# The last LayerNorm of a decoder layer: its mean taken from row sums of the last weights, its squares on ScalarE

## The chip, the cores and the metric

The kernel runs on one core of a Trainium2 chip. The metric is the time of one execution on the device in microseconds (us), the median of several runs. Profiles are single executions; their span runs from the first to the last instruction, and the execution's own time is a little longer.

## What is computed

One post-norm decoder layer on 256 positions of width 1024, in float32. The change touches its end: the down projection of the feed-forward block and the second LayerNorm.

```python
u = causal_dwconv(x @ w_up[l], conv_w_ffn[l])
f = (jax.nn.silu(u[..., :D_FF]) * u[..., D_FF:]) @ w_down[l]
x = layer_norm(DEEPNORM_ALPHA * x + f, ln2_g[l], ln2_b[l])
```

`layer_norm` subtracts the mean of the 1024 columns, multiplies by the inverse root of the variance plus 1e-5, then by a gain `g`, and adds a bias `b`. D_FF is 2816, that is 22 tiles of 128 rows of `w_down`.

## The kernel before

All weights stream in as chunks of 1 MB into three `raw` buffers (SP issues the transfers, L175). A chunk holds two units of 128x1024 numbers. Each unit is split into a high half `wh` (ScalarE, `split_h`, L192) and a low half `wl` (VectorE, `split_l`, L197), and every matrix product is three float32r matmuls: high by high, high by low, low by high (`mm3`, L305 to L307).

In the feed-forward stage `slot` runs through a list `seq` of units. A unit's two halves are made some four or five places ahead of the matmuls that read them, with the convolution, SiLU and split of the activations (`FFN`, stages 0 to 3, L817 to L851) between them. The results are the f tiles, high and low half, read as weights by the down projection. Every engine works through its queue in order, in the order in which the program issues.

The down projection accumulates four PSUM banks `dacc[t][nh]`, two blocks of 128 positions (t) by two halves of 512 columns (nh). The last eight units (`TAIL`) are taken apart: `finish(0)` multiplies them into block 0 with a slot after each; then, on VectorE, block 0 is normed: two `residual` calls (L757 adds alpha times x1, L759 takes statistics), `norm_stats` (L735 mean and variance on VectorE, L736 power of -0.5 on GpSimd), and `norm_apply` twice (L740, L741), each followed by an output transfer on SP (L997). While VectorE does this, TensorE goes on with `finish(1)`: the eight units into columns 0 to 511 of block 1, then, by `down_part`, into columns 512 to 767 and last into 768 to 1023, each in a bank of its own (`e`). `dacc[1][1]` has the earlier units' part of columns 512 to 1023. VectorE adds each bank to the residual (L990) and takes statistics (L991). After the last of them come mean and variance (L735), the power (L736), the first step (subtract the mean, multiply by g, L747) and the second step (multiply by the inverse root, add b, L744) with two output transfers, 640 columns issued by SP and 384 by ScalarE's queue (L1003). `ln2` holds g and b in SBUF.

Of the kernel before, what the change touches and what calls it, by code (L numbers as in the profile page):

```python
# [24 lines left out]
NP = DFF // P  # L25
ALPHA = 2.0 ** 0.25
EPS = 1e-5
# [22 lines left out]
CHUNK = 2048  # L50
# [3 lines left out]
TAIL = 8  # L54
# [83 lines left out]
def layer_kernel(ctx: ExitStack, tc: tile.TileContext, x, wpack, cpack, ln1_g, ln1_b, ln2_g, ln2_b, out):  # L138
    nc = tc.nc

    cst = ctx.enter_context(tc.tile_pool(name="cst", bufs=1))
    big = ctx.enter_context(tc.tile_pool(name="big", bufs=1))
    wp = ctx.enter_context(tc.tile_pool(name="wp", bufs=1))
    tmp = ctx.enter_context(tc.tile_pool(name="tmp", bufs=1))
# [5 lines left out]
    def acc_bank(name):  # L150
        return psum.tile([P, 512], F32, tag="acc", name=name)
# [4 lines left out]
    def scratch(shape, name, bufs=None, tag="scr"):  # L156
        return tmp.tile(shape, F32, tag=tag, name=name, bufs=bufs or 6)
# [4 lines left out]
    RAW_BUFS, HL_BUFS = 3, 9  # L162
    chunks, plan_units, U = plan()
# [5 lines left out]
    def issue_dma(c):  # L169
        while len(raws) <= c and len(raws) < len(chunks):  # L170
# [5 lines left out]
            if i == XR_CHUNK:  # L176
                nc.sync.dma_start(xr, x[0].rearrange("(t p) d -> p t d", p=P))

    def alloc(u, part, tag):
        k, n = units[u]["shape"]  # L180
        units[u][part] = wp.tile([P, k, n], F32R, tag=tag, name=f"{tag}{u}", bufs=HL_BUFS)
# [6 lines left out]
    def split_h(u):  # L188

        issue_dma(units[u]["chunk"] + RAW_BUFS - 1)  # L190
        alloc(u, "h", "wh")
        nc.scalar.activation(units[u]["h"], raw_of(u), AF.Copy)  # L192

    def split_l(u):

# [3 lines left out]
    def raw_of(u):  # L199
        un = units[u]  # L200
        k, n = un["shape"]
        return raws[un["chunk"]][:, un["off"]:un["off"] + k * n].rearrange("p (k n) -> p k n", k=k)
# [15 lines left out]
    def hl_split(h, l, src, eng=None):  # L218
        nc.scalar.activation(h, src, AF.Copy)  # L219
        (eng or nc.vector).tensor_tensor(l, src, h.bitcast(F32), op=ALU.subtract)  # L220
# [25 lines left out]
    neghalf = cst.tile([P, 1], F32, name="neghalf")  # L246
    nc.gpsimd.memset(neghalf, -0.5)
    neghalf2 = cst.tile([P, 1], F32, name="neghalf2")
    invf = cst.tile([P, 8], F32, name="invf")
    for i, f in enumerate(INV_FREQ):  # L250
        nc.gpsimd.memset(invf[:, i:i + 1], f)
# [7 lines left out]
    xT = big.tile([P, KT, 2, S], F32R, tag="xT", name="xT")  # L259
# [12 lines left out]
    cs = cst.tile([P, 2, 2, 8], F32, name="cs")  # L272
# [375 lines left out]
    for j in range(16):  # L648
        u = U[("g", 0)] + j
# [26 lines left out]
    def ps_pair(name):  # L676
        return pairs.tile([P, 2, 512], F32, tag="pair", name=name)
# [54 lines left out]
    def norm_stats(r, stats, pieces):  # L732

        mv = tmp.tile([P, 4], F32, tag="mv", name="mv", bufs=4)
        nc.vector.bn_aggr(mv[:, 0:2], stats[:, 0:pieces, :])  # L735
        nc.gpsimd.tensor_tensor(mv[:, 3:4], mv[:, 1:2], neghalf, op=ALU.pow)  # L736
        return mv

    def norm_apply(o, r, mv, g, b):
        nc.vector.scalar_tensor_tensor(o, r, mv[:, 0:1], g, op0=ALU.subtract, op1=ALU.mult)  # L740
        nc.vector.scalar_tensor_tensor(o, o, mv[:, 3:4], b, op0=ALU.mult, op1=ALU.add)  # L741

    def norm_second(r, mv, ln, cs):
        nc.vector.scalar_tensor_tensor(r[:, cs], r[:, cs], mv[:, 3:4], ln[:, 1, cs], op0=ALU.mult, op1=ALU.add)  # L744

    def norm_first(r, mv, ln, cs):
        nc.vector.scalar_tensor_tensor(r[:, cs], r[:, cs], mv[:, 0:1], ln[:, 0, cs], op0=ALU.subtract, op1=ALU.mult)  # L747

    x1 = big.tile([P, 2, D], F32, tag="rows", name="x1")
    x1T = big.tile([P, KT, 2, S], F32R, tag="xT", name="x1T")  # L750

# [4 lines left out]
    def residual(t, nh, bank, res, r, stats, piece, c0, c1):  # L756
        nc.vector.scalar_tensor_tensor(r[:, c0:c1], res[:, t, c0:c1], ALPHA, bank[:, c0 - nh * 512:c1 - nh * 512],  # L757
                                       op0=ALU.mult, op1=ALU.add)
        nc.vector.bn_stats(stats[:, piece, :], r[:, c0:c1])  # L759
        if piece == 0:  # L760
            with_eps(stats)
# [19 lines left out]
        residual(0, nh, banks[nh], xr, r1[0], st1[0], nh, nh * 512, nh * 512 + 512)  # L781
    norm1(0, r1[0], st1[0])
    nc.scalar.activation(neghalf2, neghalf, AF.Silu)
    banks = [acc_bank(f"o1{nh}") for nh in range(2)]
    for k in range(4):
        wo_rows(k, 1, banks)
# [14 lines left out]
    ln2 = big.tile([P, 2, D], F32, tag="e8", name="ln2")  # L801
# [6 lines left out]
    def f_tile(i):  # L808
        g = i // 8
        if g not in FT:  # L810
            FT[g] = big.tile([P, 8, 2, S], F32R, tag=("b16", "c16", "b16")[g], name=f"f{g}")
        return FT[g][:, i % 8]
# [62 lines left out]
    b0, r0 = up0_rows(0)  # L875
# [15 lines left out]
    dacc = [[acc_bank(f"d{t}{nh}") for nh in range(2)] for t in range(2)]  # L891

    def down(i, ts=(0, 1), nhs=(0, 1)):
        un = units[U[("dn", i // 2)] + i % 2]
        ft = f_tile(i)
        for t in ts:
            for nh in nhs:
                mm3(dacc[t][nh], ft[:, 0, t * P:(t + 1) * P], ft[:, 1, t * P:(t + 1) * P],
                    un["h"][:, 0, nh * 512:(nh + 1) * 512], un["l"][:, 0, nh * 512:(nh + 1) * 512],
                    i == 0, i == NP - 1 or (t == 1 and nh == 1 and i == NP - TAIL - 1))  # L900

    def down_part(i, bank, c):
        un = units[U[("dn", i // 2)] + i % 2]
        ft = f_tile(i)
        mm3(bank[:, 0:256], ft[:, 0, P:2 * P], ft[:, 1, P:2 * P],
            un["h"][:, 0, c * 256:(c + 1) * 256], un["l"][:, 0, c * 256:(c + 1) * 256], i == NP - TAIL, i == NP - 1)


    pending = []

    def take(n):
        out = []
        for stage, i in list(pending):
            if len(out) < n and i not in [p for _, p in out]:
                out.append((stage, i))
                pending.remove((stage, i))
        return out
# [49 lines left out]
        slot(k, stages)  # L967


    def finish(t):  # L970
        r = x1[:, t]
        stats = tmp.tile([P, 4, 6], F32, tag="stats", name=f"rstats{t}", bufs=2)
        if t == 0:
            for k in range(TAIL):
                down(NP - TAIL + k, (t,))
                slot(tail_from + k, take(2))
            assert not pending
            for nh in range(2):
                residual(t, nh, dacc[t][nh], x1, r, stats, nh, nh * 512, nh * 512 + 512)
        else:  # L980
            for i in range(NP - TAIL, NP):
                down(i, (t,), (0,))
            nc.vector.scalar_tensor_tensor(r[:, 512:1024], x1[:, t, 512:1024], ALPHA, dacc[t][1], op0=ALU.mult, op1=ALU.add)
            for c in range(2):
                residual(t, 0, dacc[t][0], x1, r, stats, c, c * 256, c * 256 + 256)
            for c in range(2, 4):
                bank = ps_pair(f"e{c}")[:, 0]
                for i in range(NP - TAIL, NP):
                    down_part(i, bank, c)
                nc.vector.tensor_tensor(r[:, c * 256:c * 256 + 256], r[:, c * 256:c * 256 + 256], bank[:, 0:256], op=ALU.add)  # L990
                nc.vector.bn_stats(stats[:, c, :], r[:, c * 256:c * 256 + 256])  # L991
        mv = norm_stats(r, stats, 2 if t == 0 else 4)
        if t == 0:
            for c in range(2):
                cc = slice(c * 512, (c + 1) * 512)
                norm_apply(r[:, cc], r[:, cc], mv, ln2[:, 0, cc], ln2[:, 1, cc])
                nc.sync.dma_start(out[0, t * P:(t + 1) * P, cc], r[:, cc])  # L997
            return
        for c in range(2):
            norm_first(r, mv, ln2, slice(c * 512, c * 512 + 512))  # L1000
        for cc, queue in ((slice(0, 640), nc.sync), (slice(640, D), nc.scalar)):
            norm_second(r, mv, ln2, cc)
            queue.dma_start(out[0, t * P:(t + 1) * P, cc], r[:, cc])  # L1003

    for t in range(2):
        finish(t)


_INS = ['x', 'ln1_g', 'ln1_b', 'ln2_g', 'ln2_b']
# [39 lines left out]
```

## Time and profile before

| | us |
|---|---|
| median of 3 runs | 367.78 |
| lowest and highest run | 367.34, 368.45 |
| the profiled execution | 367.38 |
| its span | 365.6 |

PE is TensorE's matmul, PEld its weight load, DVE is VectorE, ACT is ScalarE, POOL is GpSimd, SP is SyncE. Rows of a timeline give the start in us from the beginning of the span, the length in us, the engine, the line of the kernel, the operation, the tile written and those read with their shapes, and in brackets how long the engine had been idle and what released it. Instructions on one engine overlap at their edges, so the distance from one start to the next can be less than a length.

### The profile page before, as it was taken

The page shows a single profiled execution, that of the slowest core. Times are in us where ns is not written, and L with a number is a line of the kernel's source. Part 1 is how long each engine was busy: PE and PEld are TensorE (multiplying, and loading weights), DVE is VectorE, ACT ScalarE, POOL GpSimd, SP SyncE. Part 2 cuts the span into 40 slices and gives each one's busy share as a digit, 9 for nine tenths or more (in the row PEclk, how much of TensorE's full clock was granted, in tenths as well). Part 3 has the DMA queues.
Part 4 walks back from the last instruction along what each step waited for, and adds up shares of the span by engine and source line. Part 5 has one row for each costly group of instructions (what it writes and reads, how often), then busy time and mean ns, then how long its engine had stood idle before and what let it go on. Part 6 is the DMA issues. An engine that isn't in the chain of part 4 may idle for free.

```text
span 365.6 us, 5224 instructions
## 1 busy us (share of the span) xinstructions
PE 356.8 (98%) x1964; PEld 309.4 (85%) x1964; DVE 296.8 (81%) x510; ACT 222.7 (61%) x380; POOL 13.5 (4%) x34
## 2 busy tenths in 40 slices
PE   8999999999999999999999999999999999999991
PEld 8888888888898888888888888888888888888891
DVE  4885888779986669989769888977768697999884
ACT  4775777576977666653357676664737475767400
POOL 2000000000000003401100000000000000000000
PEclk9999999999999999999999999999999999999997
DMA  8988465335645634588160845447180917663011
GB/s 270 348 296 329 166 230 192 135 117 199 261 163 183 232 115 127 223 331 287 69 230 20 326 136 210 158 189 277 68 329 24 331 57 295 231 229 117 2 57 57
DMA packets 11240, 69.61 MB, mean 190 GB/s; under 512 B 1232, under 2 KB 1616, under 8 KB 4176
## 3 DMA queue, kind: packets, MB, share of 16 engines
q1 hardware_dynamic: 10496, 67.00, 49.6%
q0 software_dynamic: 576, 2.10, 1.7%
q8 instruction: 15, 0.25, 0.3%
q10 hardware_dynamic: 144, 0.20, 0.1%
q14 instruction: 9, 0.07, 0.1%
HBM read 68.24 MB, written 1.05 MB: 190 GB/s over the span
## 4 chain that ended last, share of the span: by engine, by line
PE 98%; DVE 1%; DVEq 0%; issue 0%
PE pb L323 20%; PE pb L330 10%; PE g L323 8%; PE d L305 5%; PE d L306 5%; PE d L307 5%; PE g L330 4%; PE y L323 4%; PE q L546 3%; PE k L546 3%; PE v L546 3%; PE b L323 2%; PE y L330 2%; PE c L323 2%; PE o L305 2%; PE o L307 2%
## 5 line engine op out<-in xcount | busy, mean ns | idle before, releaser
L197 DVE TENSOR_TENSOR wl<-raw,wh 128x1024 fp32r<-128x1024 f32 x99 | 121.1, 1225 | 26.2 <-ACT wh L192 25.8
L192 ACT ACTIVATE wh<-raw 128x1024 fp32r<-128x1024 f32 x99 | 103.6, 1054 | 28.0 <-DMA raw<-in_wpack 28.0
L323 PE MATMUL pb<-x1T,wh 128*128 128x512 f32 x320 | 76.2, 390 | 0.0
L323 PEld LDWEIGHTS pb<-x1T,wh 128*128 128x128 f32 x320 | 59.7, 188 | 12.1
L330 PEld LDWEIGHTS pb<-x1T,wl 128*128 128x128 f32 x320 | 41.0, 191 | 1.6
L330 PE MATMUL pb<-x1T,wl 128*128 128x256 f32 x320 | 41.5, 283 | 0.0
L220 DVE TENSOR_TENSOR wl<-raw,wh 128x1024 fp32r<-128x1024 f32 (+1 forms) x29 | 27.3, 982 | 7.8 <-ACT wh L219 7.5
L323 PE MATMUL g<-xT,wh 128*128 128x512 f32 x128 | 31.7, 394 | 0.0
L305 PE MATMUL d<-wh,f 128*128 128x512 f32 x80 | 31.3, 391 | 0.0
L306 PE MATMUL d<-wl,f 128*128 128x512 f32 x80 | 31.3, 391 | 0.0
L307 PE MATMUL d<-wh,f 128*128 128x512 f32 x80 | 31.1, 389 | 0.0
L219 ACT ACTIVATE wh<-raw 128x1024 fp32r<-128x1024 f32 (+1 forms) x29 | 23.7, 860 | 10.7 <-DMA raw<-in_wpack 6.6
L323 PEld LDWEIGHTS g<-xT,wh 128*128 128x128 f32 x128 | 23.2, 189 | 4.4
L835 DVE SCALAR_TENSOR_TENSOR fc<-fb,consts,fc 128x254 f32<-128x254 f32 x40 | 19.3, 483 | 1.4
L833 DVE SCALAR_TENSOR_TENSOR fc<-fb,consts,fc 128x255 f32<-128x255 f32 x40 | 19.1, 477 | 0.0
L827 ACT ACTIVATE fc<-fb,consts 128x256 f32<-128x256 f32 x40 | 18.0, 497 | 1.7 <-DVE fb L821 1.7
L817 ACT ACTIVATE fb<-pb 128x512 f32<-128x512 f32 x20 | 11.8, 589 | 9.9 <-PE pb L330 9.8
L307 PEld LDWEIGHTS d<-wh,f 128*128 128x128 f32 x80 | 15.0, 188 | 3.2
L305 PEld LDWEIGHTS d<-wh,f 128*128 128x128 f32 x80 | 15.1, 189 | 2.7
L306 PEld LDWEIGHTS d<-wl,f 128*128 128x128 f32 x80 | 15.1, 189 | 2.6
L330 PEld LDWEIGHTS g<-xT,wl 128*128 128x128 f32 x128 | 16.4, 191 | 0.6
L330 PE MATMUL g<-xT,wl 128*128 128x256 f32 x128 | 16.6, 283 | 0.0
(181 smaller groups left out, 576.8 us busy)
## 6 DMA issues: line engine op xcount, KB each, us to landing
raw<-in_wpack SPq DMA_DIRECT2D x55, 1024.0 KB, 5.0
raw<-in_wpack SPq DMA_DIRECT2D x6, 896.0 KB, 5.9
xr<-in_x SPq DMA_DIRECT2D x1, 1024.0 KB, 7.6
ln<-in_ln_g POOLq DMA_DIRECT2D x2, 512.0 KB, 5.5
ln<-in_ln_b POOLq DMA_DIRECT2D x2, 512.0 KB, 6.1
raw<-in_wpack SPq DMA_DIRECT2D x3, 256.0 KB, 3.2
raw<-in_wpack SPq DMA_DIRECT2D x1, 512.0 KB, 5.8
out<-x SPq DMA_DIRECT2D x2, 256.0 KB, 2.0
```

Source lines behind the costliest of these rows:

```text
L192: nc.scalar.activation(units[u]["h"], raw_of(u), AF.Copy)
L197: nc.vector.tensor_tensor(units[u]["l"], raw_of(u), units[u]["h"].bitcast(F32), op=ALU.subtract)
L219: nc.scalar.activation(h, src, AF.Copy)
L220: (eng or nc.vector).tensor_tensor(l, src, h.bitcast(F32), op=ALU.subtract)
L305: nc.tensor.matmul(o, ah, bh, start=start, stop=False)
L306: nc.tensor.matmul(o, ah, bl, start=False, stop=False)
L307: nc.tensor.matmul(o, al, bh, start=False, stop=stop)
L323: nc.tensor.matmul(bank, un["h"][:, k, n0:n0 + P], b[:, k].rearrange("p a s -> p (a s)"), start=k == 0, stop=False)
L330: nc.tensor.matmul(bank[:, 0:S], un["l"][:, k, n0:n0 + P], b[:, k, 0], start=False, stop=k == nk - 1)
L546: nc.tensor.matmul(banks[m][t], (xl if p == 2 else xh)[:, k, t * P:(t + 1) * P], wl if p == 1 else wh, start=k == 0 and p == 0, stop=k == ...
L833: nc.vector.scalar_tensor_tensor(c[:, 1:S], pb[:, a * S:a * S + S - 1], w_ffn(1, j), c[:, 1:S], op0=ALU.mult, op1=ALU.add)
L835: nc.vector.scalar_tensor_tensor(c[:, 2:S], pb[:, a * S:a * S + S - 2], w_ffn(0, j), c[:, 2:S], op0=ALU.mult, op1=ALU.add)
```

## The change

Block 1's sum over the last 256 columns is taken without waiting for these columns. The sum over columns of a product equals the product with the sums of the weights' rows.

- For each of the last eight units ScalarE, behind the high half, copies columns 768 to 1023 of the raw weights with an accumulator; the accumulator output is the row sum.
- After the last slot ScalarE multiplies the eight f tiles (block 1, high and low part) by their row sums into `fs`. GpSimd adds the 16 tiles in five instructions; its power for block 0 stands after the second. ScalarE and VectorE split the total into two float32r tiles, `fsr`.
- Two matmuls with a constant of ones, after the sixth matmul of the last column group, sum `fsr` over its rows into `mean`.
- VectorE makes the residual of block 1 in three parts, with row sums as accumulator output where a part is complete: columns 512 to 767, 768 to 1023 (without the last eight units) and 0 to 511. The order is after block 0's norm, as before; statistics are no longer taken there.
- After the mean, ScalarE squares the first two parts with the mean as bias, with accumulators; VectorE subtracts the mean from them and multiplies by g, into a new tile `res`; it subtracts the mean from the last part.
- After the last bank: one add, one multiply-and-sum instruction that starts from the other parts' sum, the power on GpSimd, and beside it the multiplication of the last part by g. Then the second step and the two transfers as before, from `res`.

```diff
+    LAST_UNITS = [U[("dn", i // 2)] + i % 2 for i in range(NP - TAIL, NP)]
+    rowsum = cst.tile([P, TAIL], F32, name="rowsum")
...
         nc.scalar.activation(units[u]["h"], raw_of(u), AF.Copy)
+        if u in LAST_UNITS:
+            j = LAST_UNITS.index(u)
+            nc.scalar.activation(scratch([P, 256], f"rowsum{j}", tag="gs", bufs=3), raw_of(u)[:, 0, 768:1024], AF.Copy,
+                                 accum_out=rowsum[:, j:j + 1])
...
+    nc.gpsimd.memset(ones32, 1.0)
...
+    nc.scalar.activation(ones, ones32, AF.Copy)
...
-            for c in range(2, 4):
-                bank = ps_pair(f"e{c}")[:, 0]
-                for i in range(NP - TAIL, NP):
-                    down_part(i, bank, c)
-                nc.vector.tensor_tensor(r[:, c * 256:c * 256 + 256], r[:, c * 256:c * 256 + 256], bank[:, 0:256], op=ALU.add)
-                nc.vector.bn_stats(stats[:, c, :], r[:, c * 256:c * 256 + 256])
...
-        for c in range(2):
-            norm_first(r, mv, ln2, slice(c * 512, c * 512 + 512))
-        for cc, queue in ((slice(0, 640), nc.sync), (slice(640, D), nc.scalar)):
-            norm_second(r, mv, ln2, cc)
-            queue.dma_start(out[0, t * P:(t + 1) * P, cc], r[:, cc])
...
+    fs = big.tile([P, TAIL, 2, P], F32, tag="d8", name="fs")
+    for j in range(TAIL):
+        nc.scalar.activation(fs[:, j], f_tile(NP - TAIL + j)[:, :, P:2 * P].bitcast(F32), AF.Copy, scale=rowsum[:, j:j + 1])
+
+    def fs_add(a, b):
+        nc.gpsimd.tensor_tensor(a, a, b, op=ALU.add)
+
+    fs_add(fs[:, 0:2], fs[:, 4:6])
+    fs_add(fs[:, 2:4], fs[:, 6:8])
...
+    mv = norm_stats(r0, stats, 2)
+    fs_add(fs[:, 0:2], fs[:, 2:4])
+    fs_add(fs[:, 0], fs[:, 1])
+    fs_add(fs[:, 0, 0], fs[:, 0, 1])
+    for c in range(2):
+        cc = slice(c * 512, (c + 1) * 512)
+        norm_apply(r0[:, cc], r0[:, cc], mv, ln2[:, 0, cc], ln2[:, 1, cc])
+        nc.sync.dma_start(out[0, 0:P, cc], r0[:, cc])
...
+    cols3 = (slice(0, 512), slice(512, 768), slice(768, D))
...
+    for c in (1, 2, 0):
+        bank = dacc[1][1][:, 256 * c - 256:256 * c] if c else dacc[1][0]
+        nc.vector.scalar_tensor_tensor(part[c], x1[:, 1, cols3[c]], ALPHA, bank, op0=ALU.mult, op1=ALU.add,
+                                       accum_out=None if c == 1 else sums[:, c:c + 1])
+    fsr = big.tile([P, 2, P], F32R, tag="xT", name="fsr")
+    hl_split(fsr[:, 0], fsr[:, 1], fs[:, 0, 0])
+    bank = ps_pair("e2")[:, 0]
+    for i in range(NP - TAIL, NP):
+        down_part(i, bank, 2)
+    nc.vector.scalar_tensor_tensor(part[1], bank[:, 0:256], 1.0, part[1], op0=ALU.mult, op1=ALU.add, accum_out=sums[:, 1:2])
+    nc.vector.tensor_reduce(sums[:, 3:4], sums[:, 0:3], axis=mybir.AxisListType.X, op=ALU.add)
+    bank = ps_pair("e3")[:, 0]
+    mean = acc_bank("mean")
+    for i in range(NP - TAIL, NP):
+        down_part(i, bank, 3)
+        if i == NP - TAIL + 1:
+            for part_hl in range(2):
+                nc.tensor.matmul(mean[:, 0:2], fsr[:, part_hl], ones, start=part_hl == 0, stop=part_hl == 1)
+
+    for c, f in ((4, -1.0 / D), (5, -1.0 / (32 * D))):
+        nc.vector.tensor_scalar(sums[:, c:c + 1], mean[:, 0:1], sums[:, 3:4], f, op0=ALU.add, op1=ALU.mult)
+    res = wp.tile([P, CHUNK], F32, tag="raw", name="res", bufs=RAW_BUFS)
+    for c in range(2):
+        nc.scalar.activation(scratch([P, 512], f"sq{c}")[:, 0:cols3[c].stop - cols3[c].start], part[c], AF.Square,
+                             bias=sums[:, 5:6], scale=1.0 / 32, accum_out=sums[:, 6 + c:7 + c])
+        nc.vector.scalar_tensor_tensor(res[:, cols3[c]], part[c], sums[:, 4:5], ln2[:, 0, cols3[c]], op0=ALU.add, op1=ALU.mult)
+    nc.vector.tensor_scalar(part[2], part[2], sums[:, 4:5], None, op0=ALU.add)
+    nc.vector.tensor_scalar(sums[:, 8:9], sums[:, 6:7], sums[:, 7:8], EPS, op0=ALU.add, op1=ALU.add)
+    nc.vector.tensor_tensor(part[2], part[2], bank[:, 0:256], op=ALU.add)
+    nc.vector.tensor_tensor_reduce(out=scratch([P, 256], "sq2"), in0=part[2], in1=part[2], scale=1.0 / D, scalar=sums[:, 8:9],
+                                   op0=ALU.mult, op1=ALU.add, accum_out=sums[:, 9:10])
+    nc.gpsimd.tensor_tensor(sums[:, 10:11], sums[:, 9:10], neghalf, op=ALU.pow)
+    nc.vector.scalar_tensor_tensor(res[:, cols3[2]], part[2], 1.0, ln2[:, 0, cols3[2]], op0=ALU.mult, op1=ALU.mult)
+    for cc, queue in ((slice(0, 640), nc.sync), (slice(640, D), nc.scalar)):
+        nc.vector.scalar_tensor_tensor(res[:, cc], res[:, cc], sums[:, 10:11], ln2[:, 1, cc], op0=ALU.mult, op1=ALU.add)
+        queue.dma_start(out[0, P:2 * P, cc], res[:, cc])
```

More of the change, by code (lines that the diff above doesn't have):

```diff
@@ L248, in layer_kernel @@
     neghalf2 = cst.tile([P, 1], F32, name="neghalf2")
+    ones32 = cst.tile([P, 2], F32, name="ones32")
+    nc.gpsimd.memset(ones32, 1.0)
+    ones = cst.tile([P, 2], F32R, name="ones")
     invf = cst.tile([P, 8], F32, name="invf")
@@ L741, in norm_apply @@
         nc.vector.scalar_tensor_tensor(o, o, mv[:, 3:4], b, op0=ALU.mult, op1=ALU.add)
[L743 to L747, printed above, removed]
     x1 = big.tile([P, 2, D], F32, tag="rows", name="x1")
@@ L967, in layer_kernel @@
         slot(k, stages)
[L970 to L980, printed above, removed]
-            for i in range(NP - TAIL, NP):
-                down(i, (t,), (0,))
-            nc.vector.scalar_tensor_tensor(r[:, 512:1024], x1[:, t, 512:1024], ALPHA, dacc[t][1], op0=ALU.mult, op1=ALU.add)
-            for c in range(2):
-                residual(t, 0, dacc[t][0], x1, r, stats, c, c * 256, c * 256 + 256)
-            for c in range(2, 4):
-                bank = ps_pair(f"e{c}")[:, 0]
-                for i in range(NP - TAIL, NP):
-                    down_part(i, bank, c)
[L990 to L999, printed above, removed]
-            norm_first(r, mv, ln2, slice(c * 512, c * 512 + 512))
-        for cc, queue in ((slice(0, 640), nc.sync), (slice(640, D), nc.scalar)):
-            norm_second(r, mv, ln2, cc)
-            queue.dma_start(out[0, t * P:(t + 1) * P, cc], r[:, cc])
@@ L1005, in layer_kernel @@
-    for t in range(2):
-        finish(t)
+    for k in range(TAIL):
+        down(NP - TAIL + k, (0,))
+        slot(tail_from + k, take(2))
+    assert not pending
+    fs = big.tile([P, TAIL, 2, P], F32, tag="d8", name="fs")
[5 more added lines that the diff above has]
+    fs_add(fs[:, 2:4], fs[:, 6:8])
@@ new lines, in layer_kernel @@
+    r0 = x1[:, 0]
+    stats = tmp.tile([P, 4, 6], F32, tag="stats", name="rstats", bufs=2)
+    for nh in range(2):
+        residual(0, nh, dacc[0][nh], x1, r0, stats, nh, nh * 512, nh * 512 + 512)
+    mv = norm_stats(r0, stats, 2)
[6 more added lines that the diff above has]
+        nc.sync.dma_start(out[0, 0:P, cc], r0[:, cc])
@@ new lines, in layer_kernel @@
+    cols3 = (slice(0, 512), slice(512, 768), slice(768, D))
+    part = [scratch([P, cc.stop - cc.start], f"part{c}") for c, cc in enumerate(cols3)]
+    sums = tmp.tile([P, 12], F32, tag="sums", name="sums", bufs=1)
+    for i in range(NP - TAIL, NP):
+        down(i, (1,), (0,))
+    for c in (1, 2, 0):
+        bank = dacc[1][1][:, 256 * c - 256:256 * c] if c else dacc[1][0]
+        nc.vector.scalar_tensor_tensor(part[c], x1[:, 1, cols3[c]], ALPHA, bank, op0=ALU.mult, op1=ALU.add,
+                                       accum_out=None if c == 1 else sums[:, c:c + 1])
@@ new lines, in layer_kernel @@
+    fsr = big.tile([P, 2, P], F32R, tag="xT", name="fsr")
[7 more added lines that the diff above has]
+    mean = acc_bank("mean")
+    for i in range(NP - TAIL, NP):
+        down_part(i, bank, 3)
+        if i == NP - TAIL + 1:
+            for part_hl in range(2):
+                nc.tensor.matmul(mean[:, 0:2], fsr[:, part_hl], ones, start=part_hl == 0, stop=part_hl == 1)
```

## The prediction

> **What bounds the kernel now.** I read the page first (busy time and the chain of waits), then the end of the chain in order of time, then the timeline of each engine from 318 us on.
>
> ```profile
> span 365.6 us, 5224 instructions
> PE 356.8 (98%) x1964; PEld 309.4 (85%) x1964; DVE 296.8 (81%) x510; ACT 222.7 (61%) x380; POOL 13.5 (4%) x34
> PE 98%; DVE 1%; DVEq 0%; issue 0%
> ```
>
> TensorE sets the pace until its last matmul; nothing the change does elsewhere counts before that, unless TensorE has to wait for it. After that matmul the chain belongs to VectorE:
>
> ```profile
> 357.84 0.43 DVE x L990
> 358.29 0.44 DVE rstats L991
> 358.75 0.27 DVE mv L735
> 359.05 1.45 DVE x L747 x2
> 360.59 0.89 DVE x L744
> 361.48 0.53 DVEq L1045
> ```
>
> Columns are start, length, what. From the last matmul's result (357.84) to the first second-step instruction that feeds an output transfer (360.59) are 2.75 us: add the bank, statistics, mean and variance, first step over all 1024 columns, and only then the second step. The second step and the two transfers stay as they are, so only these 2.75 us can shrink. The last two column groups on TensorE, and the moment at which VectorE sees a finished bank:
>
> ```profile
> 351.89 0.28 PE L305 MATMUL e<-wh,f 128*128 128x256 f32 x1
> 354.64 0.28 PE L307 MATMUL e<-wh,f 128*128 128x256 f32 x1
> 354.96 0.42 DVE L990 TENSOR_TENSOR x<-x,e 128x256 f32<-128x256 f32 x1 [0.34 <-PE e L307]
> 355.36 0.28 PE L307 MATMUL e<-wh,f 128*128 128x256 f32 x1
> 355.48 0.28 PE L305 MATMUL e<-wh,f 128*128 128x256 f32 x1
> 357.52 0.28 PE L307 MATMUL e<-wh,f 128*128 128x256 f32 x1
> ```
>
> The 24 matmuls of the first group start at 351.89 to 354.64, one per 0.12 us. The bank is visible 0.04 us after the last has ended (354.64 + 0.28 = 354.92, used at 354.96). The new mean matmuls stand after six matmuls of the last group, that is ahead of the one at 355.48: this is the time by which their operand must be there.
>
> **The new end, step by step.** Call s the time when VectorE sees the last bank (357.84 before). After the change it then does: one add (next dependent start 0.45 later, as 357.84 to 358.29), the square-and-sum with its accumulator read, the power on GpSimd, the second step. The square-and-sum is the operation that the attention masks use:
>
> ```profile
> 54.70 0.42 DVE L401 CUSTOM_DVE_ANT_0 sm<-s,mask 128x256 f32<-128x256 f32 x1
> 55.04 0.08 DVE L401 DVE_READ_ACCUMULATOR2_ANT st<- 128x1 f32 x1
> 359.09 0.55 POOL L736 TENSOR_TENSOR mv<-mv,neghalf 128x1 f32<-128x1 f32 x1 [9.32 <-DVE mv L735]
> 175.31 0.75 DVE L740 SCALAR_TENSOR_TENSOR x<-xr,mv,ln 128x512 f32<-128x512 f32 x1
> 175.36 1.12 POOL L736 TENSOR_TENSOR mv<-mv,neghalf 128x1 f32<-128x1 f32 x1 [9.33 <-DVE mv L735]
> 176.52 0.75 DVE L741 SCALAR_TENSOR_TENSOR x<-x,mv,ln 128x512 f32<-128x512 f32 x1 [0.46 <-POOL mv L736]
> ```
>
> It and its read take 0.42 in all (54.70 to 55.12), so the variance is there at s + 0.87. The power starts 0.07 later (mean and variance 358.75 + 0.27 = 359.02, power 359.09) and takes 0.55; the consumer starts 0.04 after it (175.36 + 1.12 = 176.48, then 176.52). That puts the second step at s + 1.53. But the scaling by the gain runs on VectorE beside the power, reading two SBUF tensors, and in the rows at 175 such an instruction held the power until it ended at 176.06; the power then needed 0.42. The scaling would end no later than s + 1.21, giving s + 1.67 at worst. I take 1.65: 2.75 - 1.65 = **1.10 us gained**, bounds 1.08 and 1.22.
>
> For that to hold, both partial squares must be summed before s. The mean matmul ends near 355.48 + 0.12 + 0.28 = 355.88; two one-element instructions lead to about 356.2. ScalarE then squares 512 and 256 columns with accumulators:
>
> ```profile
> 56.50 0.49 ACT L412 ACTIVATE sm<-sm,st 128x256 f32<-128x256 f32 x1
> 56.99 0.50 ACT L412 ACTIVATE sm<-sm,st 128x256 f32<-128x256 f32 x1
> 57.39 0.19 ACT L412 ACTIVATION_READ_ACCUMULATOR sm<-sm,st 128x1 f32 x1
> 339.15 0.89 ACT L827 ACTIVATE fc<-fb,consts 128x256 f32<-128x256 f32 x2
> ```
>
> 256 columns with accumulator cost 0.49 from start to start and 0.59 to the end of the read; 512 columns some 0.70 (estimate: 0.2 more, as 512 columns would take twice the part that grows). The sums end near 357.5, 0.3 before s. VectorE's gain scaling of those columns, the subtraction and the epsilon (about 0.67 + 0.42 + 0.35 + 0.1 from 356.1) end near 357.65. Both are hidden by the 18 matmuls still running, with 0.2 to 0.3 us to spare; were ScalarE 0.5 us later, s would slip by 0.2.
>
> **TensorE's own addition.** Two matmuls of 2 columns, each with a 128x128 weight load. No row shows such a matmul. The 0.12 us between the last group's matmuls bounds it above unless weights can't be fetched ahead; nothing bounds it below but zero. I take 2 x 0.12 = 0.24 us, bounds 0 to 0.4 (each load alone on the path). It stands ahead of s, so it is a loss in full.
>
> **What must be ready for the mean.** ScalarE scales eight f tiles by the row sums, GpSimd adds them in five instructions, ScalarE and VectorE split the result. The start is the last f tile:
>
> ```profile
> 343.59 0.42 ACT L847 ACTIVATE f<-ff 128x256 fp32r<-128x256 f32 x1 [0.95 <-DVE ff L844]
> 133.49 0.74 POOL L693 TENSOR_TENSOR m<-m 128x256 f32<-128x256 f32 x1 [130.89 <-DVE m L692]
> 349.18 0.78 DVE L740 SCALAR_TENSOR_TENSOR x<-x,mv,ln 128x512 f32<-128x512 f32 x1
> 349.22 0.55 POOL L736 TENSOR_TENSOR mv<-mv,neghalf 128x1 f32<-128x1 f32 x1 [172.74 <-DVE mv L735]
> 351.50 0.75 DVE L741 SCALAR_TENSOR_TENSOR x<-x,mv,ln 128x512 f32<-128x512 f32 x1
> 352.17 0.68 DVE L983 SCALAR_TENSOR_TENSOR x<-x,d 128x512 f32<-128x512 f32 x1
> ```
>
> Scalings follow each other in 0.40 (the pair of 0.89 above: 0.89 - 0.49): from 343.9 the sixth ends at 346.4, the eighth at 347.2. GpSimd's add of 256 columns costs 0.74; 512 columns lie between 0.74 (nothing grows) and 1.48 (all grows). I take the upper end, since memory-to-memory adds should grow with size: adds at 346.5 and 347.9 end at 349.4. The power of block 0 stands behind them and ends at 349.95 in place of 349.77. Then 1.48 + 0.74 + 0.37 bring 352.6, the split (0.5 on ScalarE, at most 0.42 on VectorE) 353.5. On VectorE block 0's four norm instructions end at 352.25 plus the power's 0.2, the three residual sums (about 0.4, 0.4, 0.7) near 354.0, the low half of the split 354.4. Needed: 355.48. Left alone, there is 1.1 us to spare and the wait costs nothing. What the low half holds up on VectorE, being in order, is the add of the next bank at 354.96, also not late.
>
> **They are not left alone.** GpSimd's adds and VectorE's norm steps get in each other's way:
>
> ```profile
> 152.21 1.22 DVE L197 TENSOR_TENSOR wl<-raw,wh 128x1024 fp32r<-128x1024 f32 x1
> 154.18 0.78 POOL L693 TENSOR_TENSOR m<-m 128x256 f32<-128x256 f32 x1 [0.80 <-DVE m L692]
> 154.28 1.76 DVE L197 TENSOR_TENSOR wl<-raw,wh 128x1024 fp32r<-128x1024 f32 x1
> ```
>
> The same subtraction takes 1.22, but 1.76 when it starts 0.10 after a GpSimd add of 256 columns: it lost 0.54, all of the add that was left. The rows at 175 show the reverse. After block 0's power, three norm instructions of 0.75 (x and the parameters, both in SBUF) meet 2.59 us of adds. If VectorE goes first, its residual sums (one operand in PSUM) then run beside the adds and the split ends near 355.5: no loss. If GpSimd goes first and they alternate, VectorE waits for all three adds: norms end at 354.75, sums at 356.2, split at 356.5, and TensorE stops for 1.05 us. With the power itself held too (0.45 more) it is 1.5. I take 0.3: nearer the low end, because the 512 add is priced at its upper bound and the consumer starts only 0.04 after the power.
>
> The Trainium skill, "SBUF — State Buffer", section "Who interferes with whom", states the rule that speaks against this change: a VectorE instruction with two SBUF inputs and a GpSimd instruction that reads SBUF exclude each other for a whole instruction, and whichever starts first wins. The 1.76 and the 1.12 agree. With the rule the loss is 0 to 1.5 by order; without it, none, and the gain would be 0.86.
>
> **Row sums and leftovers.** Eight row sums of 256 columns with accumulator, at 0.49 to 0.68 each, come behind the last eight weight copies on ScalarE, which is idle there:
>
> ```profile
> 328.10 0.42 ACT L847 ACTIVATE f<-ff 128x256 fp32r<-128x256 f32 x1 [1.47 <-DVE ff L844]
> 338.83 0.42 ACT L847 ACTIVATE f<-ff 128x256 fp32r<-128x256 f32 x1 [1.23 <-DVE ff L844]
> 341.27 0.42 ACT L840 ACTIVATE fs<-fc 128x256 f32<-128x256 f32 x1 [0.28 <-DVE fc L835]
> 344.61 0.42 DVE L851 TENSOR_TENSOR f<-ff,f 128x256 fp32r<-128x256 f32 x1
> 345.32 0.19 PEld L307 LDWEIGHTS d<-wh,f 128*128 128x128 f32 x1
> ```
>
> Each pair of units has 1.23 to 1.47 us of idleness before the f copy, and a pair of row sums takes 0.98 to 1.36. The last pair splits over 0.28 and 0.95. VectorE decides when ScalarE may go on, so I cost this at nothing; the cover is thin, as the last low half ends at 345.03 and its weight load is due at 345.32. A raw buffer is also read by the row sum, but VectorE's later subtraction frees it. The constants are written when those engines wait anyway; no transfer is added.
>
> **Sum.** Gain 1.10, less 0.24 and 0.30: 0.56 us. Span 365.6 to 365.0; the profiled run 367.38 to 366.8. Its time lies 0.40 under the median of the three runs (367.78), which would become 367.2. I predict **366.9**, between the two.
>
> **Rivals.** (1) The exclusion takes the gain: a stop of 0.9 to 1.5 us at the mean matmul makes of the 0.86 a loss of 0.0 to 0.6, 367.4 to 368.0. For it: both rows above, and six instructions that meet. Against: VectorE may win each time. (2) Slower: TensorE stands at the mean matmul because GpSimd's tree is long. Place: the matmul due at 355.48. It decides from a last add ending after 354.7, then costs a microsecond per microsecond. At twice my prices the adds end at 349.5, 352.4, then (power, 352.95) 355.9, 357.4 and 358.1, the split at 358.9: 3.4 us lost against 0.86 gained, 369.9. For it: no row has a 512-column add. Against: 0.74 would have to become 2.96. (3) All goes well: no stop, weights fetched ahead, 1.22 less 0.05: 366.2. (4) The change doesn't do what it says: the mean is early but ScalarE's squares end last, as if they took 0.7 more: 0.5 of the gain goes, 367.3.
>
> **How the numbers follow.** Forecast 0.50; exclusion 0.20; long tree 0.11; all well 0.14; squares last 0.05. A measurement here can tell about 0.3%, 1.1 us, from no change. The forecast case spans gains of 0.2 to 1.0, and with run-to-run scatter of half a microsecond 0.07 of it passes 1.1, as does 0.13 of "all well": faster 0.20. Slower: the long tree and a tail of the exclusion, 0.12. The rest, 0.68, within 0.3%. The range runs from 366.1 (all well) to 368.2 (the exclusion at its worst, with scatter), leaving out the long tree.
>
> **What would show it.** Right: the last matmul ends 0.2 to 0.6 us later than 357.80, one add and one square-and-sum follow, and the second step starts about 1.65 after s. TensorE's gap before the mean matmuls measures the exclusion; VectorE's block-0 norm instructions longer than 0.78 show who went first. Row sums wrong: a gap on TensorE before 346. Wrong altogether: adds of 512 columns above 2 us, or an idle VectorE ahead of its last add, waiting for ScalarE.

## The result

| | before | changed |
|---|---|---|
| median of 21 runs, us | 367.34 | 366.66 |
| lowest and highest, us | 366.79, 368.81 | 366.21, 367.19 |
| the profiled execution and its span, us | 367.38, 365.6 | 367.10, 365.2 |

The ratio of the times is 0.9978, 95% interval 0.9972 to 0.9985: the changed kernel is 0.55 to 1.0 us faster. The interval doesn't reach 1, so the gain is clear of the scatter of 21 runs, and it is less than the 0.3% that the prediction took for the least that can be told. 366.66 lies 0.24 under the forecast 366.9.

Most of the scatter arises long before the change takes effect. The first bank of block 0 reaches VectorE at 345.97 in the profile of before, at 346.37 after, and between 345.5 and 346.8 in the runs below. In the two main profiles TensorE is 0.4 us apart as early as the first six matmuls on the inputs, which the change doesn't touch. The chain of waits of before, then of the changed kernel:

```profile
5.01 1.95 PE q L546 x6
```

```profile
5.02 2.33 PE q L557 x6
```

TensorE's part of the same chains, in before and then in the changed kernel, ahead of the first row sum (323.24 in the changed kernel):

```profile
313.44 3.65 PE pb L323 x16
```

```profile
313.83 3.65 PE pb L334 x16
```

From the start of these sixteen matmuls to the first residual are 32.53 us before and 32.54 after, and 32.53 or 32.54 in each of the nine kernels below. So the scatter lies ahead of 313 us, and the row sums, which stand between the two points, cost TensorE nothing.

So I read each profile from a fixed point, the start of that first residual, to the end of the span and to block 1's second step. The span is known to 0.1 us, so the differences below are taken from the last column:

| kernel | span, us | first residual, us | from there to the end, us | from there to the second step, us |
|---|---|---|---|---|
| before | 365.6 | 345.97 | 19.63 | 14.62 |
| changed | 365.2 | 346.37 | 18.83 | 13.82 |
| e1, no late adds | 364.9 | 346.07 | 18.83 | 13.83 |
| e2, no mean matmuls | 364.3 | 345.73 | 18.57 | 13.59 |
| e3, longer tree | 364.8 | 345.52 | 19.28 | 14.36 |
| e4, old end | 366.9 | 346.31 | 20.59 | 15.63 |
| e5, old end, split early | 366.0 | 346.15 | 19.85 | 14.85 |
| e6, mean later | 364.8 | 345.69 | 19.11 | 14.12 |
| e7, scaling first | 364.6 | 345.58 | 19.02 | 14.04 |
| e8, root on ScalarE | 364.1 | 345.79 | 18.31 | 13.31 |
| e9, the same, one mean matmul | 364.9 | 346.75 | 18.15 | 13.18 |

By this measure the change gains 0.80 us. It is made of two terms. The first, VectorE and GpSimd in the changed kernel's timeline around the last bank (start, length, engine, line, operation, tiles):

```profile
357.92 0.21 DVE L1040 TENSOR_SCALAR sums<-sums 128x1 f32<-128x1 f32 x1
358.46 0.42 DVE L1041 TENSOR_TENSOR part<-part,e 128x256 f32<-128x256 f32 x1 [0.33 <-PE e L318]
358.92 0.48 DVE L1042 CUSTOM_DVE_ANT_0 sq<-part,sums 128x256 f32<-128x256 f32 x1
359.33 0.08 DVE L1042 DVE_READ_ACCUMULATOR2_ANT sums<- 128x1 f32 x1
359.33 0.42 DVE L1045 SCALAR_TENSOR_TENSOR res<-part,ln 128x256 f32<-128x256 f32 x1
359.49 0.67 POOL L1044 TENSOR_TENSOR sums<-sums,neghalf 128x1 f32<-128x1 f32 x1 [5.97 <-DVE sums L1042]
360.19 1.42 DVE L1047 SCALAR_TENSOR_TENSOR res<-res,sums,ln 128x640 f32<-128x640 f32 x2 [0.44 <-POOL sums L1044]
```

From the last bank (358.46) to the second step (360.19) are 1.73 us, against 2.75 before: 1.02 gained. VectorE waits 0.33 for the bank, so the squares on ScalarE were in time, and 0.44 for the power, which is now what the second step waits for. The second term is on TensorE, in the last column group:

```profile
355.76 0.28 PE L318 MATMUL e<-wh,f 128*128 128x256 f32 x1
355.88 0.28 PE L1030 MATMUL mean<-ones,fsr 128*128 128x2 f32 x2
356.02 0.37 PE L316 MATMUL e<-wh,f 128*128 128x256 f32 x1
356.23 0.28 PE L317 MATMUL e<-wl,f 128*128 128x256 f32 x1
```

From L318 at 355.76 to L317 at 356.23 are 0.47 us where two steps of 0.12 would be 0.24: the mean matmuls cost 0.23. There is no gap ahead of them. 1.02 less 0.23 is the 0.80, to the rounding of the rows.

The meeting of GpSimd and VectorE took place all the same. VectorE in the changed kernel's timeline, from block 0's norm to the split:

```profile
349.57 0.78 DVE L751 SCALAR_TENSOR_TENSOR x<-x,mv,ln 128x512 f32<-128x512 f32 x1
350.45 1.60 DVE L752 SCALAR_TENSOR_TENSOR x<-x,mv,ln 128x512 f32<-128x512 f32 x1
351.98 1.22 DVE L751 SCALAR_TENSOR_TENSOR x<-x,mv,ln 128x512 f32<-128x512 f32 x1
353.23 0.84 DVE L752 SCALAR_TENSOR_TENSOR x<-x,mv,ln 128x512 f32<-128x512 f32 x1
355.27 0.28 DVE L228 TENSOR_TENSOR fsr<-fs,fsr 128x128 fp32r<-128x128 f32 x1
```

and the chain of waits of the same kernel, which lists GpSimd's adds one by one (start, length, what):

```profile
349.62 0.55 POOL mv L747
350.17 1.34 POOL fs L989
351.58 1.08 POOL fs L989
352.73 0.79 POOL fs L989
```

GpSimd goes first, and they alternate: the add from 350.17 ends at 351.51 and VectorE's instruction at 352.05, the add of 256 columns at 352.66, the next norm instruction at 353.20, the last add at 353.52, the last norm instruction at 354.07. Three instructions of 0.75 became 1.60, 1.22 and 0.84. The split ends at 355.55, and TensorE comes to the mean matmuls at 355.88: 0.33 us to spare. This chain is followed back through GpSimd's queue and then shows 5.93 us of "issue" (time in which an engine waited for nothing that the profile shows) from 353.52 to the power; the timeline shows what that hides, VectorE and TensorE at work.

### The profile page after: what moved, and what is told of

The parts are those of the page before. It is cut to its first block, busy times and chain, and to the rows that moved or that the text cites. A ratio compares the mean times of both kernels' runs of the same rounds, so it can differ in the third digit from the quotient of the medians.

```text
span 365.2 us, 5276 instructions
## 1 busy us (share of the span) xinstructions
PE 357.4 (98%) x1966; PEld 309.8 (85%) x1966; DVE 298.4 (82%) x516; ACT 230.0 (63%) x410; POOL 18.7 (5%) x40
## 3 DMA queue, kind: packets, MB, share of 16 engines
HBM read 68.24 MB, written 1.05 MB: 190 GB/s over the span
## 4 chain that ended last, share of the span: by engine, by line
PE 95%; issue 2%; DVE 1%; POOL 1%; POOLq 0%; DVEq 0%
PE pb L334 20%; PE pb L341 10%; PE g L334 8%; PE d L316 4%; PE d L317 4%; PE d L318 4%; PE g L341 4%; PE y L334 4%; PE q L557 3%; PE v L557 3%; PE k L557 3%; PE b L334 2%; PE y L341 2%; PE c L334 2%; PE h L334 2%; PE o L317 2%
## 5 line engine op out<-in xcount | busy, mean ns | idle before, releaser
L317 PE MATMUL d<-wl,f 128*128 128x512 f32 x80 | 31.3, 391 | 0.0
L318 PE MATMUL d<-wh,f 128*128 128x512 f32 x80 | 31.1, 389 | 0.0
L318 PEld LDWEIGHTS d<-wh,f 128*128 128x128 f32 x80 | 15.0, 188 | 3.2
L317 PEld LDWEIGHTS d<-wl,f 128*128 128x128 f32 x80 | 15.1, 188 | 2.6
L827 DVE TENSOR_TENSOR fb<-pb,fb 128x512 f32<-128x512 f32 x20 | 13.7, 686 | 4.0 <-ACT fb L823 3.9
```

The lines of the kernel that those rows point to most:

```text
L317: nc.tensor.matmul(o, ah, bl, start=False, stop=False)
L318: nc.tensor.matmul(o, al, bh, start=False, stop=stop)
```

## The experiments

**e1: without the last three adds.** The three lines are left out, so that the sum holds 2 of the 16 tiles.

```diff
     mv = norm_stats(r0, stats, 2)
-    fs_add(fs[:, 0:2], fs[:, 2:4])
-    fs_add(fs[:, 0], fs[:, 1])
-    fs_add(fs[:, 0, 0], fs[:, 0, 1])
```

> The last three GpSimd adds are left out, so the mean lacks 14 of the 16 tiles and the output is not the reference's. Theory (the meeting of GpSimd's adds with block 0's norm is absorbed: the low half of the split ends 0.33 us ahead of the mean matmul): block 0's norm instructions shrink from 1.60, 1.22, 0.84 to about 0.75 each, the residual sums start about 1.4 us earlier, and the time stays that of the changed kernel, about 0.75 us under before (0.1 either way). Rival (the meeting costs time on the path): a further 0.3 us faster, about 1.05 us under before.

Block 0's norm on VectorE:

```profile
350.16 0.75 DVE L752 SCALAR_TENSOR_TENSOR x<-x,mv,ln 128x512 f32<-128x512 f32 x1
350.83 0.75 DVE L751 SCALAR_TENSOR_TENSOR x<-x,mv,ln 128x512 f32<-128x512 f32 x1
351.61 0.75 DVE L752 SCALAR_TENSOR_TENSOR x<-x,mv,ln 128x512 f32<-128x512 f32 x1
353.56 0.29 DVE L228 TENSOR_TENSOR fsr<-fs,fsr 128x128 fp32r<-128x128 f32 x1
```

All at 0.75, the split 1.4 us earlier, and 18.83 us from the first residual to the end, the changed kernel's own figure. The runs give 0.9984 of before (0.9971 to 0.9997), too wide to add anything. The adds lengthen VectorE's norm, and none of it reaches the end.

**e2: without the mean matmuls.** The mean lacks the last eight units' part of the last 256 columns.

```diff
-    mean = acc_bank("mean")
     for i in range(NP - TAIL, NP):
         down_part(i, bank, 3)
-        if i == NP - TAIL + 1:
-            for part_hl in range(2):
-                nc.tensor.matmul(mean[:, 0:2], fsr[:, part_hl], ones, start=part_hl == 0, stop=part_hl == 1)
...
-        nc.vector.tensor_scalar(sums[:, c:c + 1], mean[:, 0:1], sums[:, 3:4], f, op0=ALU.add, op1=ALU.mult)
+        nc.vector.tensor_scalar(sums[:, c:c + 1], sums[:, 3:4], sums[:, 3:4], f, op0=ALU.add, op1=ALU.mult)
```

> The two mean matmuls are left out, so the mean lacks the last eight units' part of the last 256 columns. Theory (they cost TensorE 0.23 us in full, as the trace of the changed kernel shows 0.35 us between two neighbours that are 0.12 apart elsewhere): 24 matmuls of the last group 0.12 apart throughout, the time 0.23 us under the changed kernel, about 1.0 us under before. Rival (they are hidden in the pipeline and the trace's gap is a modelled end): no difference from the changed kernel.

The second step comes 13.59 us after the first residual, 0.23 under the changed kernel; the time is 0.9971 (0.9959 to 0.9982) of before. The 0.23 is real and in full on the path.

**e3: a longer tree.**

```diff
     fs_add(fs[:, 0], fs[:, 1])
+    fs_add(fs[:, 4:6], fs[:, 6:8])
     fs_add(fs[:, 0, 0], fs[:, 0, 1])
```

> One more GpSimd add of 512 columns (1.3 us), whose result nobody reads, ahead of the last add. Theory (0.33 us of spare time ahead of the mean matmul, then a microsecond per microsecond): the split ends 0.9 to 1.3 us later, TensorE stops 0.6 to 1.0 us ahead of the mean matmuls, and the time is 0.6 to 1.0 us over the changed kernel, about level with before. Rival (the wait is hidden, or the split waits for VectorE and not for GpSimd): less than 0.2 us over the changed kernel.

TensorE, and VectorE's last norm instruction and split:

```profile
354.91 0.28 PE L318 MATMUL e<-wh,f 128*128 128x256 f32 x1
355.03 0.17 PE L1031 MATMUL mean<-ones,fsr 128*128 128x2 f32 x1
355.58 0.27 PE L1031 MATMUL mean<-ones,fsr 128*128 128x2 f32 x1 [0.39 <-DVE fsr L228]
352.38 1.67 DVE L752 SCALAR_TENSOR_TENSOR x<-x,mv,ln 128x512 f32<-128x512 f32 x1
355.25 0.28 DVE L228 TENSOR_TENSOR fsr<-fs,fsr 128x128 fp32r<-128x128 f32 x1
```

TensorE stops between the two mean matmuls, for the low half of the split, and the second step is 0.54 us later than in the changed kernel (14.36); the time is that of before, 0.9998 (0.9986 to 1.0011). The stop is less than the expected 0.6 to 1.0: VectorE's last norm instruction grew from 0.84 to 1.67, and it is this 0.83 that the split is late by, not the 1.3 of the add: VectorE's last norm instruction now waits for the new add of 512 columns in place of the last one of 128, and that one runs beside the residual sums, which keep their length (0.74 and 0.68, as in the changed kernel). Less the 0.33 to spare, 0.5 remains. The rival was half right: the split waits for VectorE, but the wait isn't hidden.

**e4: the old end beside the new work.** All added work is kept, its results unused, and block 1 ends as before. In short:

```diff
-    part = [scratch([P, cc.stop - cc.start], f"part{c}") for c, cc in enumerate(cols3)]
...
+    for c in range(2):
+        residual(1, 0, dacc[1][0], x1, r, stats, c, c * 256, c * 256 + 256)
     hl_split(fsr[:, 0], fsr[:, 1], fs[:, 0, 0])
...
+        nc.vector.bn_stats(stats[:, c, :], r[:, c * 256:c * 256 + 256])
+    mv = norm_stats(r, stats, 4)
```

> All the added work (row sums, scalings, adds, split, mean matmuls) is kept with its results unused, and the end of block 1 is that of before: statistics, mean and variance, first step, second step. Theory (what is gained is gained after the last matmul alone, and the added work costs the two matmuls and nothing else): 0.2 us over before (0.1 to 0.35), with the end after the last bank at 2.75 us as before. Rival (row sums or adds also cost time by way of the other engines): 0.5 us or more over before. Other rival (the added work itself relieves something): under before.

1.0027 (1.0016 to 1.0039) of before: 1.0 us slower, not 0.2; from the first residual to the second step 15.63, 1.01 over before. VectorE and TensorE around the mean matmuls:

```profile
354.97 0.43 DVE L764 BATCH_NORM_STATS2 rstats<-x 128x6 f32<-128x256 f32 x1
355.95 0.43 DVE L764 BATCH_NORM_STATS2 rstats<-x 128x6 f32<-128x256 f32 x1
356.29 0.28 DVE L228 TENSOR_TENSOR fsr<-fs,fsr 128x128 fp32r<-128x128 f32 x1
355.82 0.17 PE L1024 MATMUL mean<-ones,fsr 128*128 128x2 f32 x1
356.62 0.27 PE L1024 MATMUL mean<-ones,fsr 128*128 128x2 f32 x1 [0.63 <-DVE fsr L228]
```

The split stands on VectorE behind block 1's statistics. They make it end at 356.57, 0.75 after the first mean matmul. So this kernel doesn't price the added work; it prices it together with a wait that the changed kernel escapes by taking no statistics. The next kernel takes the wait away.

**e5: the same with the split ahead of the statistics.**

```diff
+    hl_split(fsr[:, 0], fsr[:, 1], fs[:, 0, 0])
     for i in range(NP - TAIL, NP):
         down(i, (1,), (0,))
...
-    hl_split(fsr[:, 0], fsr[:, 1], fs[:, 0, 0])
```

> As e4_old_end (all added work, unused, and the end of before), but the split of the tile sum stands on VectorE ahead of block 1's residual and statistics. In e4 the statistics, 0.9 us ahead of the split on VectorE, made TensorE stop 0.68 us at the mean matmuls. Theory (the added work costs the two matmuls, 0.23 us, and the wait only where VectorE comes to the split too late): no stop, from block 0's first bank on VectorE to the end of the span 19.85 us (before 19.63, e4 20.59), time 0.2 us over before. Rival (the row sums and adds cost time by themselves): 20.3 us or more.

VectorE's split and second step:

```profile
353.77 0.28 DVE L228 TENSOR_TENSOR fsr<-fs,fsr 128x128 fp32r<-128x128 f32 x1
361.00 1.41 DVE L1032 SCALAR_TENSOR_TENSOR x<-x,mv,ln 128x640 f32<-128x640 f32 x2
```

19.85 to the end, as expected, and 14.85 to the second step, 0.23 over before; in the runs 1.0000 (0.9991 to 1.0009), an interval that reaches 0.3 us either way and so doesn't contradict 0.2. The scalings and adds cost nothing, and the row sums ahead of the first residual cost nothing either (32.53 us, as above); the added work costs the two matmuls. This kernel also prices the new end: it does the changed kernel's added work and ends as before, and its second step is 1.03 us later than the changed kernel's, which is the 1.02 read above.

**e6: the mean later.**

```diff
-        if i == NP - TAIL + 1:
+        if i == NP - TAIL + 3:
```

> The two mean matmuls stand after twelve matmuls of the last column group in place of six, 0.72 us later. Theory (ScalarE's squares and VectorE's subtraction then end 0.72 later, 0.4 us after the last bank, since the changed kernel has 0.33 us between the epsilon instruction's end and the last add): the last add waits for ScalarE's sum and starts 0.35 to 0.45 us after the bank is there; from block 0's first bank to the end 19.2 us (changed kernel 18.83). Rival (those steps have more room): 18.8 us.

VectorE, and TensorE's last matmul (which ends at 357.75):

```profile
357.47 0.28 PE L318 MATMUL e<-wh,f 128*128 128x256 f32 x1
357.96 0.21 DVE L1040 TENSOR_SCALAR sums<-sums 128x1 f32<-128x1 f32 x1
358.09 0.41 DVE L1041 TENSOR_TENSOR part<-part,e 128x256 f32<-128x256 f32 x1
```

The last add starts at 358.09 where the bank was there at 357.79: 0.30 late, and so is the second step (14.12). A little under the expected 0.35 to 0.45, because the add starts 0.13 after the epsilon instruction's start and need not wait for its end. The mean has about 0.4 us of room (358.46 - 357.92 - 0.13) as the changed kernel places it. This kernel and e7 were executed once each, so only their profiles are read.

**e7: the scaling first.** The multiplication of the last part by the gain (L1045) is moved ahead of the square-and-sum (L1042).

> The multiplication of the last part by the gain stands ahead of the square-and-sum in place of beside the power. Theory (beside the power it holds the power up by 0.12 us, which took 0.67 and not 0.55, but ahead it costs its whole 0.35): the power takes 0.55 us, the second step starts 1.96 us after the last add's start (changed kernel 1.73), the time is 0.2 us over the changed kernel. Rival (the 0.12 has another cause): the power still takes 0.67.

```profile
357.68 0.42 DVE L1041 TENSOR_TENSOR part<-part,e 128x256 f32<-128x256 f32 x1 [0.33 <-PE e L318]
359.04 0.55 POOL L1045 TENSOR_TENSOR sums<-sums,neghalf 128x1 f32<-128x1 f32 x1 [6.31 <-DVE sums L1043]
359.62 1.42 DVE L1047 SCALAR_TENSOR_TENSOR res<-res,sums,ln 128x640 f32<-128x640 f32 x2 [0.66 <-POOL sums L1045]
```

With nothing beside it the power takes 0.55, and the second step comes 1.94 after the add, 0.21 later than in the changed kernel. The 0.12 is the price of the neighbour; a neighbour is still cheaper than the 0.35 ahead.

**e8: the root on ScalarE.** ScalarE is idle after its squares. An instruction on a constant makes ScalarE load the table of this function ahead of time, and the root of the variance follows on the same engine.

```diff
+    nc.scalar.activation(neghalf2, ones32[:, 0:1], AF.Abs_reciprocal_sqrt)
     nc.vector.tensor_scalar(part[2], part[2], sums[:, 4:5], None, op0=ALU.add)
...
-    nc.gpsimd.tensor_tensor(sums[:, 10:11], sums[:, 9:10], neghalf, op=ALU.pow)
+    nc.scalar.activation(sums[:, 10:11], sums[:, 9:10], AF.Abs_reciprocal_sqrt)
```

> The inverse root of block 1's variance is taken by ScalarE (its table is loaded behind the squares, by an instruction on a constant) in place of the power on GpSimd. Theory (after the last matmul every step is on the path, so what the power's 0.16 + 0.67 + 0.03 shrink to is gained): the second step starts 1.2 to 1.35 us after the last add's start (changed kernel 1.73); from block 0's first bank to the end 18.35 to 18.45 us; 0.4 us under the changed kernel, about 1.1 under before. Rival (the table load ends after the variance is there, or the gain multiplication is then the bound): 0.1 us or less under the changed kernel.

```profile
357.32 1.28 ACT L1039 ACT_TABLE_LOAD   x1
358.62 0.20 ACT L1039 ACTIVATE neghalf<-ones 128x1 f32<-128x1 f32 x1
358.86 0.20 ACT L1045 ACTIVATE sums<-sums 128x1 f32<-128x1 f32 x1
357.88 0.42 DVE L1042 TENSOR_TENSOR part<-part,e 128x256 f32<-128x256 f32 x1 [0.33 <-PE e L318]
358.75 0.42 DVE L1046 SCALAR_TENSOR_TENSOR res<-part,ln 128x256 f32<-128x256 f32 x1
359.10 1.41 DVE L1048 SCALAR_TENSOR_TENSOR res<-res,sums,ln 128x640 f32<-128x640 f32 x2
```

The root is there at 359.06, the table having been loaded in time (358.60), and the second step starts 1.22 after the add, right behind the gain multiplication. So the expectation's rival had the next bound right, and not its price: the multiplication (0.35 from start to start) now ends as late as the root. From the first residual to the second step are 13.31 us, 0.51 under the changed kernel; the time is 0.9956 (0.9942 to 0.9970) of before, that is 1.1 to 2.1 us faster. The changed kernel's interval, 0.9972 to 0.9985 of before, doesn't overlap this one.

**e9: the root on ScalarE and one mean matmul.** The low half of the split, its VectorE instruction and the second mean matmul are left out, so that the sum behind the mean is rounded once.

```diff
-    hl_split(fsr[:, 0], fsr[:, 1], fs[:, 0, 0])
+    nc.scalar.activation(fsr[:, 0], fs[:, 0, 0], AF.Copy)
...
-            for part_hl in range(2):
-                nc.tensor.matmul(mean[:, 0:2], fsr[:, part_hl], ones, start=part_hl == 0, stop=part_hl == 1)
+            nc.tensor.matmul(mean[:, 0:2], fsr[:, 0], ones, start=True, stop=True)
```

> As e8_root_scalar, and the mean takes one matmul with the tile sum rounded to float32r once: the low half of the split, its VectorE instruction and the second mean matmul are left out, so the last eight units' part of the mean is less exact. Theory (of the two matmuls' 0.23 us one half goes, and nothing else stands there): the matmul after the mean starts 0.12 us earlier against its neighbours, from block 0's first bank to the end 18.2 us (e8 18.31), 0.1 us under e8. Rival (the first mean matmul carries the whole cost, the change of shape): no difference from e8.

```profile
356.14 0.28 PE L318 MATMUL e<-wh,f 128*128 128x256 f32 x1
356.26 0.17 PE L1029 MATMUL mean<-ones,fsr 128*128 128x2 f32 x1
356.49 0.28 PE L317 MATMUL e<-wl,f 128*128 128x256 f32 x1
```

0.35 from L318 to L317, so one such matmul costs 0.11, half of two. From the first residual to the second step are 13.18 us, 0.13 under e8. The runs can't tell the two apart: 0.9959 (0.9944 to 0.9973).

## Why the prediction was right, and where a step was off

- **The sum.** 0.56 us gained was forecast, 0.80 came by the profiles and 0.55 to 1.0 by the runs. Range and sign held. The difference is the stop of 0.30 that didn't come, less 0.08 that the new end fell short. That 366.9 is so near 366.66 is in part luck: it takes 367.46 as the time of before, where 21 runs give 367.34, and two errors of opposite sign stand in the sum.
- **The new end.** Forecast 1.65 from bank to second step, measured 1.73. The square-and-sum with its read took 0.49 (358.92 to 359.41) where the masks' rows gave 0.42; the rest was as priced. The power was held up by the scaling beside it, as the rows at 175 us had suggested, by 0.12 (e7: 0.67 against 0.55); with 1.67 as the worst case I had allowed for that, so the excess is the square-and-sum's. The 1.02 gained lies just under the bounds of 1.08 and 1.22.
- **TensorE's own addition.** 0.24 forecast, 0.23 measured, in the changed kernel's rows and by e2.
- **Squares hidden.** Yes; 0.2 to 0.3 us of room was forecast, 0.4 is there (e6).
- **Row sums at no cost.** Yes: 32.54 us of TensorE with them, 32.53 without. ScalarE's idle time before the last f copy fell from 0.95 to 0.41 us, and the f tile was not late. That copy in the changed kernel's timeline:

```profile
342.91 0.42 ACT L853 ACTIVATE f<-ff 128x256 fp32r<-128x256 f32 x1 [0.41 <-DVE ff L850]
```

- **The stop at the mean matmul: the term that was mis-sized.** I put it at 0.30 and it was 0. The reason given was half wrong. I took the alternating order with GpSimd ahead to be the costly branch (norms to 354.75, a stop of 1.05), and VectorE going first to be what would spare us. The trace shows the alternating order, with GpSimd ahead, and still no stop: the norms end at 354.07, on before's clock (0.40 earlier) 353.67. I had let every instruction begin from nothing when the other released it. Measured, VectorE's instructions end 0.54 to 0.55 after the release, not 0.75, and GpSimd's adds 0.61 and 0.32, not the priced 0.74 and 0.37: some of the held instruction's time overlaps the other's. The three norm instructions make 0.6 of the 1.08 between 354.75 and 353.67. The 512-column add also took 1.34 and not 1.48, and the power ended at 349.77 (on before's clock) and not at 349.95, since the first two adds, which began 1.1 earlier than priced and took 2.53 together in place of 2.96, were done before it; begun at the priced 346.5 they would have ended at 349.03, still ahead of the power at 349.22. Another 0.27 came behind the norm: the residual sums took 1.28 and not 1.45, the low half of the split 0.20 and not 0.3. The prediction's own rows showed this already: the subtraction of 1.76 began when 0.68 of the add was left (154.28 to 154.96) and lost 0.54, not all of it as I wrote, and the power at 175 needed 0.42 after its release where one left alone takes 0.55. The exclusion itself is there: e1 shows the norm at 0.75 without the adds. The 0.30 was a compromise between a branch of 0 and one of 1.05; the kernel took the second branch's order and came to the first one's price.
- **The rule of the Trainium skill** ("SBUF — State Buffer", section "Who interferes with whom"): the direction agrees, and 1.60 for 0.75 is its sharpest sign here. For two SBUF inputs this section of the Trainium skill says that the two contend; that the second blocks fully for the whole instruction it says of VectorE's two-port modes, and the prediction carried this over. Taken to mean that the held instruction needs its full length after the release, that doesn't agree with the 0.54 measured. The traces don't tell whether the held instruction begins before the other ends or the other frees it early.
- **The rivals.** The long tree has the right place and the right kind of price (e3, e4), but counts from VectorE's split and not from GpSimd's last add. "All goes well" was nearest in the stop and wrong about the weights: each mean matmul costs its 0.11. The exclusion's rival is right that the instructions alternate and wrong about the price. The squares were not last: the mean has 0.4 us of room (e6).

What stays open: the scatter of a microsecond, which lies ahead of 313 us and which I did not follow, and whether block 0's power ever loses to VectorE (see the last section).

## What to carry to other kernels

Once the pacing engine has run out of work, every dependent step is on the path, down to a single-column power, and an engine that is idle by then can be a cheaper place for it (e8: 0.51 us for one moved instruction and one that loads its table ahead of time). A value that can be known early pays only if what makes it is in time on every queue that it passes: the mean was in time because VectorE no longer took statistics ahead of it, was late by 0.75 us when it did (e4), and was in time again with its split queued ahead of the statistics (e5). Find how much room such a wait has by delaying it on purpose, not from the sum of the parts.

## What the runs showed that I had not expected

Instructions that exclude each other do so for less than their length: a VectorE instruction of 0.75 us that had been held up ended 0.54 to 0.55 us after the release, every time (350.17 + 1.34 to 352.05, 352.66 to 353.20, 353.52 to 354.07). Who goes first seems to hang on less than the rows can tell. The power at 175 us, which took 1.12 in before, in the changed kernel:

```profile
175.73 0.78 DVE L751 SCALAR_TENSOR_TENSOR x<-xr,mv,ln 128x512 f32<-128x512 f32 x1
175.78 0.56 POOL L747 TENSOR_TENSOR mv<-mv,neghalf 128x1 f32<-128x1 f32 x1 [9.31 <-DVE mv L746]
```

It starts 0.05 after VectorE in both; it takes 1.12 again in e8 and e9 and 0.56 in e1 to e7, though the change doesn't touch this place. Block 0's power, 0.04 to 0.05 behind VectorE, took 0.55 in all eleven profiles. Had it lost, the prediction's 0.45 for a held power would meet 0.33 us to spare; no run shows that.

A matmul with 2 moving columns costs 0.11 us, nearly the 0.12 of one with 256 between the same neighbours, so that a "free" matmul of almost no columns costs as much as a narrow one.
